# 32 latent tokens fewer in the dense expert path of each layer, gathered instead, with u and v rows side by side

## The chip, the cores and the metric

The kernel runs on one core of one Trainium2 chip. The metric is the device time of one execution, in microseconds, and less is better. All times are of this one core.

## The reference, cut to what matters

The reference is a stack of two layers over 512 latent tokens and 256 context tokens of 1024 features. Each layer has a token mixer (gated recurrences and short convolutions) and then an expert mixer. Only the expert mixer is touched here:

```python
cand = (s1[..., :, None] + s2[..., None, :]).reshape(bsz, t, PEER_HEADS, n_cand)
cidx = (i1[..., :, None] * N_KEYS + i2[..., None, :]).reshape(bsz, t, PEER_HEADS, n_cand)
top, pos = lax.top_k(cand, PEER_TOPK)
eidx = jnp.take_along_axis(cidx, pos, axis=-1)
gate = jax.nn.softmax(top, axis=-1).astype(h.dtype)
def block(args):
    hk, ek, gk = args
    act = jax.nn.gelu(jnp.einsum('ted,td->te', u[ek], hk), approximate=False)
    return jnp.einsum('te,ted->td', gk * act, v[ek])
```

Each token picks 8 x 16 = 128 of 16384 experts. An expert is one row of u and one row of v, of 1024 numbers each. For each picked expert the token's features are multiplied with the row of u, the sum goes through a GELU and is scaled with the gate, and that number scales the row of v. The sum over the 128 experts is added to the token's features. In the last layer the context does not pass the expert mixer, since nothing reads it any more.

## The kernel before, in words

Tokens are held transposed: 128 partitions of features, eight chunks, tokens along the free axis. `peer` (a layer's expert mixer) serves tokens in blocks of 128, in one of two ways.

The dense way computes all 16384 experts for the token, and multiplies those that it didn't pick with a gate of zero. Layer 0 does so for all four latent blocks (nt = 512 tokens) and layer 1 for three (nt = 384). Matrices are split into a high and a low part, so each product is three matmuls (lines 302 to 304 for u, in `experts_in`; 818 to 820 for v, in `dense`): 6144 matmuls of nt columns per layer. Each 512 KB tile of weights is loaded by SyncE (line 291), rounded by ScalarE to the high part (`whi`, line 293), and VectorE subtracts it for the low part (`wlo`, line 295). The gates of a block are built in `gates` out of one-hot matrices, in groups of 32 tokens: `oB` is built by VectorE for the first ND tokens of eight (line 757) and by ScalarE for the others (lines 761, 762), `oA` by VectorE (lines 765, 768), and small matmuls (line 773) join them. The result goes to DRAM (`gd`). Beside this stage some of the experts' activations are computed ahead (34 pairs of tiles in layer 0, 30 in layer 1) and parked in DRAM (`ad`). The dense stage then loads gates and parked activations, multiplies them (line 807), splits them (lines 810, 811), and adds the products with v to the residual (line 822).

The gathering way fetches only the picked rows. Layer 0 does so for the two context blocks and layer 1 for the last latent block. In `gather_block` partition p is token p, and slot e fetches the row of the e-th picked expert of each token: one indirect DMA of 128 rows of 4 KB, issued by GpSimd (line 854). A first loop over 128 slots fetches rows of u and takes the dot product with the token's features on VectorE (line 861). One GELU on ScalarE serves all slots. A second loop fetches rows of v and accumulates them on VectorE (line 870). Buffers are `gr` (3) and, in every fourth slot, `gs` (1). Buffers of `gs` come from a pool that opens behind the gate stage, so U0 = 96 says how many slots of the first context block may use `gr` alone and so start early, during the gate stage. At the end the sums are transposed by TensorE (line 875) and added to the residual (line 877).

The order of each engine's instructions is fixed when the program is built, by a scheduler that works from its own estimates. Dense and gathering work are interleaved on VectorE's queue by it. An engine executes its queue in order, so an instruction that waits holds up those behind it.

## Time and profile before

| what | value |
|---|---|
| median of 3 runs (lowest to highest) | 4181.68 us (4173.64 to 4183.18) |
| the profiled execution: time, and its span | 4183.52 us, 4181.8 us |
| TensorE matmuls busy | 3942.6 us (94%) |
| TensorE weight loads busy | 3419.5 us (82%) |
| VectorE busy | 3392.2 us (81%) |
| ScalarE busy | 1747.0 us (42%) |
| GpSimd busy | 1203.1 us (29%) |
| DMA moved | 984.54 MB, mean 235 GB/s |

The shares are means over the whole span, and the stages differ. The expert mixer of layer 0 has its top-k from about 600 us, its gate stage from 917, its dense stage from 1300 to 2419; in layer 1 the gate stage runs from 3015 to 3267 and the dense stage to 4125. The first stretch up to 600 us and that from 2440 to 2840 us are the token mixers. Weight loads overlap the matmuls. The DMA share is the mean busy share of the 16 DMA engines.

### The profile page before, as it was taken

The page shows a single profiled execution, that of the slowest core. Times are in us where ns is not written, and L with a number is a line of the kernel's source. Part 1 is how long each engine was busy: PE and PEld are TensorE (multiplying, and loading weights), DVE is VectorE, ACT ScalarE, POOL GpSimd, SP SyncE. Part 2 cuts the span into 40 slices and gives each one's busy share as a digit, 9 for nine tenths or more (in the row PEclk, how much of TensorE's full clock was granted, in tenths as well). Part 3 has the DMA queues.
Part 4 walks back from the last instruction along what each step waited for, and adds up shares of the span by engine and source line. Part 5 has one row for each costly group of instructions (what it writes and reads, how often), then busy time and mean ns, then how long its engine had stood idle before and what let it go on. Part 6 is the DMA issues. An engine that isn't in the chain of part 4 may idle for free.

```text
span 4181.8 us, 59060 instructions
## 1 busy us (share of the span) xinstructions
PE 3942.6 (94%) x21357; PEld 3419.5 (82%) x21357; DVE 3392.2 (81%) x6672; ACT 1747.0 (42%) x2919; POOL 1203.1 (29%) x924
## 2 busy tenths in 40 slices
PE   7999999999996999999999989989999999999995
PEld 4888868878885777877777768867999999999994
DVE  4766639989997999888888878758986688888886
ACT  4444332347774222222222245433599433333331
POOL 0211100033331244555555612210000024444443
PEclk9999999999998999999999999989999999999997
DMA  6444122379998899989989821112467679999996
GB/s 224 141 148 154 60 71 81 116 270 322 322 324 278 299 329 356 319 314 323 326 318 324 312 96 56 66 61 92 146 213 220 217 260 344 343 342 343 344 333 212
DMA packets 382164, 984.54 MB, mean 235 GB/s; under 512 B 30384, under 2 KB 161712, under 8 KB 377520
## 3 DMA queue, kind: packets, MB, share of 16 engines
q1 hardware_dynamic: 271280, 578.06, 40.1%
q0 software_dynamic: 110592, 402.70, 27.2%
q8 instruction: 169, 2.77, 0.3%
q14 instruction: 123, 1.01, 0.1%
HBM read 883.39 MB, written 97.26 MB: 235 GB/s over the span
## 4 chain that ended last, share of the span: by engine, by line
PE 50%; DVE 18%; issue 13%; DMA 10%; POOL 6%; ACT 2%; SPq 0%; POOLq 0%; DVEq 0%; ACTq 0%
PE pj L302 5%; PE p L820 5%; POOL gr L854 5%; PE pj L303 5%; PE pj L304 5%; PE p L818 5%; PE p L819 5%; PE p L302 4%; PE p L303 4%; PE p L304 4%; DMA gr<-in_v,picki 4%; DVE wlo L295 3%; PE gps L773 2%; DMA gr<-in_u,picki 2%; DVE acc L870 2%
## 5 line engine op out<-in xcount | busy, mean ns | idle before, releaser
L293 ACT ACTIVATE whi<-wraw 128x1024 fp32r<-128x1024 f32 x624 | 657.2, 1060 | 1266.8 <-PE p L819 568.7
L854 POOL DMA_INDIRECT gr<-in_u,picki x312 | 410.7, 1316 | 1545.7 <-DVE picki L828 634.9
L295 DVE TENSOR_TENSOR wlo<-wraw,whi 128x1024 fp32r<-128x1024 f32 x624 | 762.0, 1225 | 109.2 <-ACT whi L293 107.5
L818 PE MATMUL p<-Wh,whi 128*128 128x512 f32 (+1 forms) x2048 | 738.6, 366 | 38.5 <-ACT Wh L810 20.1
L820 PE MATMUL p<-Wh,wlo 128*128 128x512 f32 (+1 forms) x2048 | 747.5, 367 | 18.3 <-DVE wlo L295 18.1
L819 PE MATMUL p<-Wl,whi 128*128 128x512 f32 (+1 forms) x2048 | 749.1, 366 | 16.0 <-DVE Wl L811 15.9
L302 PE MATMUL p<-hxh,whi 128*128 128x512 f32 (+1 forms) x2048 | 751.7, 367 | 0.0
L303 PE MATMUL p<-hxl,whi 128*128 128x512 f32 (+1 forms) x2048 | 749.9, 366 | 0.0
L304 PE MATMUL p<-hxh,wlo 128*128 128x512 f32 (+1 forms) x2048 | 749.4, 367 | 0.0
L854 POOL DMA_INDIRECT gr<-in_v,picki x288 | 393.1, 1365 | 426.1 <-DVE acc L870 313.3
L818 PEld LDWEIGHTS p<-Wh,whi 128*128 128x128 f32 x2048 | 387.2, 190 | 89.0 <-ACT Wh L810 22.9
L820 PEld LDWEIGHTS p<-Wh,wlo 128*128 128x128 f32 x2048 | 388.1, 190 | 72.9 <-DVE wlo L295 32.4
L861 DVE SCALAR_TENSOR_TENSOR gr<-gr,htok 128x1024 f32<-128x1024 f32 x312 | 378.5, 1221 | 80.2 <-DMA gr<-in_u,picki 79.2
L819 PEld LDWEIGHTS p<-Wl,whi 128*128 128x128 f32 x2048 | 388.3, 190 | 64.1 <-DVE Wl L811 23.5
L304 PEld LDWEIGHTS p<-hxh,wlo 128*128 128x128 f32 x2048 | 386.3, 189 | 39.5 <-DVE wlo L295 0.6
L302 PEld LDWEIGHTS p<-hxh,whi 128*128 128x128 f32 x2048 | 386.2, 189 | 38.6
L303 PEld LDWEIGHTS p<-hxl,whi 128*128 128x128 f32 x2048 | 385.9, 188 | 38.8
L870 DVE SCALAR_TENSOR_TENSOR acc<-gr,gw,acc 128x1024 f32<-128x1024 f32 x285 | 365.4, 1282 | 54.5 <-DMA gr<-in_v,picki 52.7
L810 ACT ACTIVATE Wh<-A 128x1024 fp32r<-128x1024 f32 (+1 forms) x128 | 122.2, 955 | 368.9 <-DVE A L807 309.8
L302 PE MATMUL pj<-h512h,whi 128*128 128x512 f32 x640 | 262.0, 412 | 12.3 <-ACT whi L293 4.6
L773 PE MATMUL gps<-oA,oB 128*128 128x128 f32 x1792 | 253.3, 279 | 18.6 <-DVE oA L765 9.1
L773 PEld LDWEIGHTS gps<-oA,oB 128*128 128x128 f32 x1792 | 242.9, 193 | 31.6 <-ACT oB L762 8.4
(315 smaller groups left out, 6608.9 us busy)
## 6 DMA issues: line engine op xcount, KB each, us to landing
wraw<-in_ut SPq DMA_DIRECT2D x256, 512.0 KB
wraw<-in_vt SPq DMA_DIRECT2D x256, 512.0 KB
gd<-stg SPq DMA_DIRECT2D x28, 2048.0 KB
wmod<-in_w_mod SPq DMA_DIRECT2D x96, 512.0 KB
wraw<-in_w_in SPq DMA_DIRECT2D x64, 512.0 KB
gt<-gd SPq DMA_DIRECT2D x32, 1024.0 KB
gt<-gd SPq DMA_DIRECT2D x32, 768.0 KB
ad<-A SPq DMA_DIRECT2D x34, 512.0 KB
```

What stands on the lines that cost most here:

```text
L293: nc.scalar.activation(hi, raw, AF.Copy)
L295: nc.vector.tensor_tensor(lo, raw, hi.bitcast(F), op=OP.subtract)
L302: nc.tensor.matmul(out, wh[:, k], ah[:, k, :n], start=i == 0, stop=False)
L303: nc.tensor.matmul(out, wh[:, k], al[:, k, :n], start=False, stop=False)
L304: nc.tensor.matmul(out, wl[:, k], ah[:, k, :n], start=False, stop=i == KC - 1)
L773: nc.tensor.matmul(pt[:, s], B[:, s4 + s], A[:, s4 + s], start=True, stop=True)
L818: nc.tensor.matmul(pt, hi[:, j], wh, start=j == 0, stop=False)
L819: nc.tensor.matmul(pt, hi[:, j], wl, start=False, stop=False)
L820: nc.tensor.matmul(pt, lo[:, j], wh, start=False, stop=j == NG - 1)
L854: nc.gpsimd.indirect_dma_start(out=t, out_offset=None, in_=src, in_offset=bass.IndirectOffsetOnAxis(ap=eidx[:, e:e + 1], axis=0))
L861: nc.vector.scalar_tensor_tensor(u, u, 1.0, htok, op0=OP.mult, op1=OP.mult, accum_out=act[:, e:e + 1])
L870: nc.vector.scalar_tensor_tensor(acc, v, w[:, e:e + 1], acc, op0=OP.mult, op1=OP.add)
```

## The change

In each layer the last 32 latent tokens of the dense tokens (REST) leave the dense path: nt is 480 in layer 0 and 352 in layer 1. They are gathered in a further call of `gather_block`, behind the other blocks, four slots to an operation: partition 32 j + i holds token i and slot group j, so that 128 slots of 32 tokens are 32 operations. A matmul with `pack` (four stacked unit matrices) adds the four groups as it transposes.

For all gathers, u and v are laid side by side in DRAM, so one indirect DMA fetches 128 rows of 8 KB. There is one loop: fetch a slot, take the dot product, GELU and gate scale for this slot on ScalarE, and accumulate the previous slot. Buffers are two `gr` and two `gs` of 8 KB per partition. U0 is 24, ND is 3 instead of 4 (ScalarE builds five of eight rows of `oB`), and the last block's gate groups are three instead of four. In `dense` the two gate multiplications become one. Tile A has two buffers in layer 0. The store of x for the next layer comes behind the gathers. Some scratch tiles share the buffers of `wlo`, and the transposing matmul of the modulation writes two columns.

```diff
-ND = 4
+ND = 3
+REST = (32, 32)
-U0 = 96
+U0 = 24
...
-                nc.tensor.matmul(pm[:, j], part[:, j * P:(j + 1) * P], self.selm, start=True, stop=True)
+                nc.tensor.matmul(pm[:, j, 0:2], part[:, j * P:(j + 1) * P], self.selm[:, 0:2], start=True, stop=True)
...
-        nt = len(db) * P
+        r = REST[l]
+        nt = len(db) * P - r
...
-                    self.gates(kp, gd, n, ahead, *self.select(kp, tbs[b], 2))
+                    sel = self.select(kp, tbs[b], 2)
+                    nq = (nt - n * P) // 32
+                    self.gates(kp, gd, n, ahead, *sel, min(nq, P // 32))
+                    if nq < P // 32:
+                        e32 = kp.tile([P, PH * TOPK], I32, name="e32", tag="ri", bufs=1)
+                        self.eidx(sel, e32)
+                        for j in range(P // r):
+                            for dst, src in ((rest[0], e32), (rest[1], sel[2])):
+                                nc.sync.dma_start(dst[j * r:(j + 1) * r], src[P - r:, j * r:(j + 1) * r])
...
+                self.gather_block(l, cp, c2, hdx[0, P - r:], *rest, TC + nt, r, 0)
                 if not last:
                     self.xd = self.dram.tile([P, KC, TX], F, name="xd")
...
-        A = ap.tile([P, 2, nt], F, name="A", tag="A", bufs=3)
+        A = ap.tile([P, 2, nt], F, name="A", tag="A", bufs=2 if l == 0 else 3)
...
-                for t in range(2):
-                    av = A[:, t].rearrange("p (c t) -> p c t", t=32)
-                    nc.vector.tensor_tensor(av, av, gt[:, :, j % 4 + t, :], op=OP.mult)
+                av = A.rearrange("p i (c t) -> p i c t", t=32)
+                gv = gt[:, :, j % 4:j % 4 + 2, :].rearrange("p c i t -> p i c t")
+                nc.vector.tensor_tensor(av, av, gv, op=OP.mult)
...
-    def gather_block(self, l, cp, c2, b, hd, eidx, gate, n0):
+    def gather_block(self, l, cp, c2, hd, eidx, gate, t0, n, n0):
         nc, a = self.nc, self.a
-        S = PH * TOPK
+        D = KC * P
+        S = PH * TOPK * n // P
...
+        def fetch(e):
+            if e < n0 or e % 4 < 2:
+                t = cp.tile([P, 2, D], F, name="gr", tag="gr", bufs=2)
             else:
+                t = c2.tile([P, 2, D], F, name="gs", tag="gs", bufs=2)
+            nc.gpsimd.indirect_dma_start(out=t.rearrange("p a d -> p (a d)"), out_offset=None, in_=a[f"uv{l}"],
                                          in_offset=bass.IndirectOffsetOnAxis(ap=eidx[:, e:e + 1], axis=0))
...
+        def dot(e, t):
+            nc.vector.scalar_tensor_tensor(t[:, 0], t[:, 0], 1.0, htok, op0=OP.mult, op1=OP.mult,
+                                           accum_out=act[:, 0, e:e + 1])
+            self.gelus[1] = nc.scalar.activation(act[:, 1, e:e + 1], act[:, 0, e:e + 1], AF.Gelu).ins
+            nc.scalar.activation(act[:, 2, e:e + 1], act[:, 1, e:e + 1], AF.Copy, scale=gate[:, e:e + 1])
...
+        prev = None
         for e in range(S):
+            t = fetch(e)
+            dot(e, t)
+            if prev is not None:
+                add(e - 1, prev)
+            prev = t
+        add(S - 1, prev)
...
+                    nc.tensor.matmul(pt, acc[:, c * P:(c + 1) * P], self.pack, start=True, stop=True)
...
-        d[f"u{l}"] = peer_u[l]
-        d[f"v{l}"] = peer_v[l]
+        d[f"uv{l}"] = np.concatenate([peer_u[l], peer_v[l]], axis=1)
```

Three places of the order tell what the diff can't. The first is VectorE's queue at the end of layer 0's dense stage. `resx<-p` is a dense addition to the residual, `acc<-gr` or `acc<-gs` an accumulation of a slot, `resc<-accT` the addition of a finished context block. Before (the second of these dense additions is the layer's last):

```order
L822 SCALAR_TENSOR_TENSOR resx<-p_18008,mod_108,resx 128x512
L295 TENSOR_TENSOR wlo<-wraw,whi 128x1024
L870 SCALAR_TENSOR_TENSOR acc<-gr,gw,acc 128x1024 x2
L822 SCALAR_TENSOR_TENSOR resx<-p_18040,mod_108,resx 128x512
L295 TENSOR_TENSOR wlo<-wraw,whi 128x1024
L870 SCALAR_TENSOR_TENSOR acc<-gr,gw,acc 128x1024
L870 SCALAR_TENSOR_TENSOR acc<-gs,gw,acc 128x1024
L877 SCALAR_TENSOR_TENSOR resc<-accT,mod_108,resc 128x128 x2
```

Now the same place (line 879 is the dot product, 889 the accumulation, 836 the dense addition):

```order
L836 SCALAR_TENSOR_TENSOR resx<-p_17965,mod_113,resx 128x480
L889 SCALAR_TENSOR_TENSOR acc<-gr,act,acc 128x1024
L879 SCALAR_TENSOR_TENSOR gs,act<-gs,htok 128x1024
L889 SCALAR_TENSOR_TENSOR acc<-gs,act,acc 128x1024
L836 SCALAR_TENSOR_TENSOR resx<-p_17997,mod_113,resx 128x480
L879 SCALAR_TENSOR_TENSOR gs,act<-gs,htok 128x1024
L889 SCALAR_TENSOR_TENSOR acc<-gs,act,acc 128x1024
L879 SCALAR_TENSOR_TENSOR gr,act<-gr,htok 128x1024
L889 SCALAR_TENSOR_TENSOR acc<-gr,act,acc 128x1024
L879 SCALAR_TENSOR_TENSOR gr,act<-gr,htok 128x1024
L889 SCALAR_TENSOR_TENSOR acc<-gr,act,acc 128x1024
```

Two accumulations stood behind the last dense addition; now 45 dot products and 45 accumulations do, in this pattern, 13 of the second context block and 32 of the new block.

The second place is TensorE's queue at the same point. `p` is a dense product, `accT` the transpose of a gathered sum, `nst` the statistics of the next layer's first norm over all 512 latent tokens, `pj` its first projection. Before:

```order
L820 MATMUL p_18040<-Wh,wlo 128x512
L237 MATMUL nst<-sq,ones_70 32x512 x7
L875 MATMUL accT<-ident,acc 128x128
L237 MATMUL nst<-sq,ones_70 32x512
L875 MATMUL accT<-ident,acc 128x128
L245 MATMUL nst_19969<-cols,npart 128x1 x4
L875 MATMUL accT<-ident,acc 128x128 x3
L221 MATMUL rb<-ident,n0r 128x128 x4
L875 MATMUL accT<-ident,acc 128x128
L302 MATMUL pj<-h512h,whi 128x512 x2
```

Now:

```order
L834 MATMUL p_17997<-Wh,wlo 128x480
L904 MATMUL accT<-ident,acc 128x128 x8
L906 MATMUL accT<-pack,acc 128x32 x2
L241 MATMUL nst<-sq,ones_70 32x512
L906 MATMUL accT<-pack,acc 128x32
L241 MATMUL nst<-sq,ones_70 32x512
L906 MATMUL accT<-pack,acc 128x32
L241 MATMUL nst<-sq,ones_70 32x512
L906 MATMUL accT<-pack,acc 128x32
```

The norm's statistics followed the last dense matmul; now the transposes of both gathered blocks stand between, and the norm's statistics follow the new block's.

The third place is the end of layer 1's dense stage on VectorE. Before:

```order
L822 SCALAR_TENSOR_TENSOR resx<-p_34461,mod_109,resx 128x384
L870 SCALAR_TENSOR_TENSOR acc<-gr,gw,acc 128x1024 x2
L822 SCALAR_TENSOR_TENSOR resx<-p_34493,mod_109,resx 128x384
L870 SCALAR_TENSOR_TENSOR acc<-gr,gw,acc 128x1024
L870 SCALAR_TENSOR_TENSOR acc<-gs,gw,acc 128x1024
L870 SCALAR_TENSOR_TENSOR acc<-gr,gw,acc 128x1024 x3
```

Now:

```order
L836 SCALAR_TENSOR_TENSOR resx<-p_34490,mod_114,resx 128x352
L908 SCALAR_TENSOR_TENSOR resx<-accT,mod_114,resx 128x32
L836 SCALAR_TENSOR_TENSOR resx<-p_34522,mod_114,resx 128x352
L908 SCALAR_TENSOR_TENSOR resx<-accT,mod_114,resx 128x32
L836 SCALAR_TENSOR_TENSOR resx<-p_34554,mod_114,resx 128x352
L215 TENSOR_SCALAR fv<-nst_35884 128x4
```

Accumulations stood behind the last dense addition; now both gathered blocks are finished ahead of it, and the final norm follows at once.

## Rows read from the trace of the kernel before

**Rows 1.** Busy time by stretch: stretch, its length, engines with instructions, TensorE clock, DMA share, GB/s.

```profile
917.00:1300.00 383.00, 362.90 (x2055) 312.80 (x2053) 351.14 (x710) 306.85 (x707) 128.33 (x101) 0.99 0.95 318
1300.00:2419.00 1119.00, 1054.67 (x4524) 853.25 (x4524) 972.57 (x1292) 297.50 (x292) 548.21 (x388) 0.98 0.90 319
3015.00:3267.00 252.00, 252.00 (x1726) 251.81 (x1726) 186.00 (x386) 235.61 (x546) 0.00 (x0) 1.00 0.67 207
3267.00:3395.00 128.00, 124.08 (x701) 121.95 (x700) 108.15 (x319) 45.65 (x49) 0.00 (x0) 0.99 0.62 206
3395.00:4125.00 730.00, 720.26 (x4112) 711.10 (x4111) 645.60 (x818) 241.58 (x255) 326.99 (x246) 1.00 0.92 337
4125.00:4151.00 26.00, 0.00 (x0) 0.00 (x0) 17.98 (x14) 0.00 (x0) 12.92 (x11) 0.54 0.76 247
4151.00:4182.00 31.00, 15.85 (x40) 5.27 (x40) 9.21 (x22) 8.62 (x13) 0.00 (x0) 0.67 0.18 68
```

**Rows 2.** Timeline of TensorE: start us, duration us, instruction; layer 0, layer 1, gate stage.

```profile
1699.73 0.39 PE L302 MATMUL p<-hxh,whi 128*128 128x512 f32 x1
...
1701.09 0.39 PE L302 MATMUL p<-hxh,whi 128*128 128x512 f32 x1
...
3700.14 0.33 PE L302 MATMUL p<-hxh,whi 128*128 128x384 f32 x1
...
3701.01 0.33 PE L304 MATMUL p<-hxh,wlo 128*128 128x384 f32 x1
...
3018.82 2.84 PE L773 MATMUL gps<-oA,oB 128*128 128x128 f32 x24
```

**Rows 3.** Timeline of VectorE: two dot products, then an accumulation and what follows it.

```profile
3707.71 1.22 DVE L861 SCALAR_TENSOR_TENSOR gr<-gr,htok 128x1024 f32<-128x1024 f32 x1
...
3708.85 1.22 DVE L861 SCALAR_TENSOR_TENSOR gr<-gr,htok 128x1024 f32<-128x1024 f32 x1
...
1560.25 1.28 DVE L870 SCALAR_TENSOR_TENSOR acc<-gr,gw,acc 128x1024 f32<-128x1024 f32 x1
1561.44 1.22 DVE L295 TENSOR_TENSOR wlo<-wraw,whi 128x1024 fp32r<-128x1024 f32 x1
```

**Rows 4.** DMA queues in 917:1300, 1300:2419, 3395:4125 (with slices), 4125:4151: packets, MB, share.

```profile
q0 software_dynamic: 14633, 53.25, 39.9%
...
q0 software_dynamic: 55850, 203.40, 51.7%
q1 hardware_dynamic: 42284, 152.90, 37.8%
...
GB/s 322 362 324 394 320 321 368 324 348 395 264 356 378 308 375 315 317 375 331 324 408 271 353 386 304 355 346 314 357 352 316 398 282 341 385 296 330 344 296 240
q0 software_dynamic: 35092, 127.80, 47.9%
q1 hardware_dynamic: 31392, 117.85, 44.0%
...
q0 software_dynamic: 1772, 6.43, 76.4%
```

**Rows 5.** Groups by line and shape: one-hot rows on ScalarE in 3015:3267; small activations, whole span.

```profile
L762 ACT ACTIVATE oB<-oB,gt,gtn 128x128 f32<-128x128 f32 x192 | 83.2, 529 | 0.0
L761 ACT ACTIVATE oB<-iota,gt 128x128 f32<-128x128 f32 x184 | 60.5, 434 | 0.0
...
L213 ACT ACTIVATE or<-os x8: 205/206/210, 187.8 to 2779.6; 128x6 f32<-128x6 f32 x4, 128x4 f32<-128x4 f32 x4
```

**Rows 6.** Timeline of VectorE behind the last dense matmul: first, last slot; last addition.

```profile
4120.67 1.31 DVE L870 SCALAR_TENSOR_TENSOR acc<-gr,gw,acc 128x1024 f32<-128x1024 f32 x1 [0.53 <-DMA gr<-in_v,picki]
...
4149.72 1.28 DVE L870 SCALAR_TENSOR_TENSOR acc<-gs,gw,acc 128x1024 f32<-128x1024 f32 x1
...
4162.43 0.35 DVE L877 SCALAR_TENSOR_TENSOR resx<-accT,mod,resx 128x128 f32<-128x128 f32 x1 [0.89 <-PE accT L875]
```

**Rows 7.** Groups by line and shape: the modulation's transposing matmul.

```profile
L191 PE MATMUL pmod<-selm,mpart 128*128 128x128 f32 x192 | 30.9, 283 | 2.7 <-ACT mpart L189 2.7
```

More of the change, by code (lines that the diff above doesn't have):

```diff
@@ L90, in setup @@
             nc.vector.tensor_copy(self.selm[q:q + 2, 0:2], self.ident[0:2, 0:2])
+        self.pack = c.tile([P, 32], F, name="pack")
+        for q in range(0, P, 32):
+            nc.vector.tensor_copy(self.pack[q:q + 32], self.ident[0:32, 0:32])
         self.res = self.streams()
@@ L227, in norm_close @@
         t0, nt, pp = nm
-        part = self.wp.tile([P, nt], F, name="npart", tag=f"np{nt}", bufs=1)
+        part = self.wp.tile([P, nt], F, name="npart", tag="wlo", bufs=3)
         self.nc.scalar.activation(part, pp, AF.Copy)
@@ L667, in peer @@
             ad = dr.tile([n_ahead, P, 2, nt], F, name="ad")
-            hd = dr.tile([len(gb), P, KC * P], F, name="hd")
+            hd = dr.tile([NCB, P, KC * P], F, name="hd")
+            hdx = hd if last else dr.tile([1, P, KC * P], F, name="hdx")
             sd = dr.tile([len(gb), PH, P, 2, P], F, name="sd")
@@ L673, in peer, with pick_bufs @@
             cp = self.pool(f"pc{l}", stack=es, side="right")
-            def pick_bufs(pool):
-                return [pool.tile([P, PH * TOPK], dt, name="pick" + n) for n, dt in (("i", I32), ("g", F))]
+            def pick_bufs(pool, n=PH * TOPK):
+                return [pool.tile([P, n], dt, name="pick" + k + str(n)) for k, dt in (("i", I32), ("g", F))]
             picks = [pick_bufs(cp) for _ in range(early)]
+            rest = pick_bufs(cp, r)
             with ExitStack() as es2:
@@ L685, in peer @@
                 self.nms = None, None
-                if last:
-                    self.norm_mod(nmx, l, 1, 0, *hx, hd=hd, b0=NB - NCB - 1)
-                else:
+                self.norm_mod(nmx, l, 1, 0, *hx, hd=hdx, b0=NB - NCB - (2 if last else 1))
+                if not last:
                     hcb = kp.tile([P, 2, KC, TC], R, name="hcb", tag="big", bufs=2)
                     hc = [hcb[:, 0], hcb[:, 1]]
-                    self.norm_mod(nmx, l, 1, 0, *hx)
                     self.norm_mod(nmc, l, 1, 1, *hc, hd=hd)
@@ L727, in peer @@
                 self.dense(l, es2, ap, gd, ad, hx, nt)
+                for n, b in enumerate(gb):
+                    if n >= early:
+                        picks.append(pick_bufs(c2))
+                        self.late_top(c2, sd[n], *picks[n])
+                    self.gather_block(l, cp, c2, hd[1 if last else n], *picks[n], b * P, P, U0 if n < early else 0)
+                self.gather_block(l, cp, c2, hdx[0, P - r:], *rest, TC + nt, r, 0)
                 if not last:
@@ L731, in peer, with gates @@
                         nc.sync.dma_start(self.xd[:, c], self.res.x[:, c])
-                for n, b in enumerate(gb):
-                    if n >= early:
-                        picks.append(pick_bufs(c2))
-                        self.late_top(c2, sd[n], *picks[n])
-                    self.gather_block(l, cp, c2, b, hd[n], *picks[n], U0 if n < early else 0)
-    def gates(self, kp, gd, n, ahead, i1, i2, gate):
+    def gates(self, kp, gd, n, ahead, i1, i2, gate, nq):
         nc = self.nc
@@ L749, in gates @@
         nc.scalar.activation(tn, tg, AF.Copy, scale=-1.0)
-        for q in range(P // 32):
+        for q in range(nq):
             stg = kp.tile([P, P, 32], F, name="stg", tag="big", bufs=2)
@@ L822, in dense, with eidx @@
                 nc.vector.scalar_tensor_tensor(dst, pt, self.mod[l][:, 5 * KC + c, 0:1], dst, op0=OP.mult, op1=OP.add)
+    def eidx(self, sel, out):
+        i1, i2, _ = sel
+        self.nc.vector.scalar_tensor_tensor(i1, i1, 128.0, i2, op0=OP.mult, op1=OP.add)
+        self.nc.vector.tensor_copy(out, i1)
     def pick(self, pool, tb, nh, eidx, gate):
-        nc = self.nc
-        i1, i2, g = self.select(pool, tb, nh)
-        nc.vector.scalar_tensor_tensor(i1, i1, 128.0, i2, op0=OP.mult, op1=OP.add)
-        nc.vector.tensor_copy(eidx, i1)
-        nc.vector.tensor_copy(gate, g)
+        sel = self.select(pool, tb, nh)
+        self.eidx(sel, eidx)
+        self.nc.vector.tensor_copy(gate, sel[2])
     def late_top(self, cp, sd, eidx, gate):
@@ L864, in gather_block @@
-        nc.vector.tensor_tensor(w, w, gate, op=OP.mult)
-        for e in range(S):
-            v = fetch(a[f"v{l}"], e)
-            if e == 0:
-                nc.vector.tensor_scalar(acc, v, w[:, e:e + 1], None, op0=OP.mult)
-            else:
-                nc.vector.scalar_tensor_tensor(acc, v, w[:, e:e + 1], acc, op0=OP.mult, op1=OP.add)
-        s = 1 if b < NCB else 0
+        def dot(e, t):
[3 more added lines that the diff above has]
+            nc.scalar.activation(act[:, 2, e:e + 1], act[:, 1, e:e + 1], AF.Copy, scale=gate[:, e:e + 1])
@@ new lines, in add @@
+        def add(e, t):
+            w = act[:, 2, e:e + 1]
+            if e == 0:
+                nc.vector.tensor_scalar(acc, t[:, 1], w, None, op0=OP.mult)
+            else:
+                nc.vector.scalar_tensor_tensor(acc, t[:, 1], w, acc, op0=OP.mult, op1=OP.add)
+        prev = None
+        for e in range(S):
+            t = fetch(e)
[4 more added lines that the diff above has]
+        add(S - 1, prev)
+        s = 1 if t0 < TC else 0
```

32 lines of the change are left out of this document (13 added, 19 removed).

## The prediction

> **What bounds the kernel now.** I read the busy time by stretches first, because the stages have different limits [rows 1]. The stretches are the gate stage of layer 0 (917 to 1300 us), its dense stage (1300 to 2419), the gate stage of layer 1 (3015 to 3267), its dense stage (3267 to 4125) and the end. In both dense stages TensorE is busy 94 to 99%, so it looks like the bound. But the DMA engines are at 0.90 to 0.92 and VectorE at 87 to 88% in the same stretches: three lanes are nearly full, and work taken off one must land on another. In the gate stage of layer 0 the DMA share is the highest of all, 0.95. In that of layer 1 TensorE and ScalarE (236 of 252 us) are both full. The last rows of the group show what an unfinished gather costs: from 4125 to 4151 TensorE does nothing.
>
> Then I read the steps from one instruction to the next. Six dense matmuls of 512 columns start within 1.36 us (1699.73 to 1701.09) and five of 384 within 0.87 (3700.14 to 3701.01) [rows 2]: steps of 227 and 174 ns. So 128 columns cost 53 ns and 32 columns 13.2 ns. On VectorE a dot product takes 1.14 us to the next instruction and an accumulation 1.19 [rows 3], so one slot (dot and add) costs 2.33 us.
>
> **The change, part by part.** I price against the profiled execution, 4183.5 us (span 4181.8); the median of the runs is 1.8 us below it.
>
> *TensorE, dense.* 6144 dense matmuls in each layer become 32 columns narrower: 2 x 6144 x 13.2 ns = 162 us of TensorE time. That is the gain if TensorE were the only bound. Below I ask stage by stage what is late next.
>
> *Added gathers.* 768 gathers of 512 KB become 448 of 1 MB: bytes rise from 403 to 470 MB. VectorE gets 64 slots more, 64 x 2.33 = 149 us.
>
> *Gate stage, layer 0 (383 us).* One group of 32 tokens of 16 falls away. TensorE: 1009 expert matmuls at 227 ns and 1024 small ones at 0.118 us [rows 2] are 350 us; after, 992 at 213.8 ns and 960 small ones are 325. The order holds 120 dot products ahead of the stage's end before and 28 slots now, so about 30 MB of gathers in place of 63; 53 MB of them took 39.9% of the stretch [rows 4]. So the DMA engines, full before, have room. ScalarE gets busier: five one-hot rows of eight instead of four, 300 pairs in place of 256, each 0.9 us by its two mean durations [rows 5], +40; fewer copies, -5; the 56 small operations of the early slots at 0.2 us [rows 5], +12: 354 of busy time. ScalarE is late next. I take 360 us, **-23** (from 345 to 383).
>
> *Dense stage, layer 0 (1119 us).* TensorE: 4512 matmuls x 213.8 ns = 965 us instead of 1024. VectorE: 973 us [rows 1], plus 79 dots and minus 36 adds that stand in this stage, +47; the two gate multiplications become one and all tiles are shorter, about -17: 1003. DMA: the gathers took 51.7% for 203 MB, or 2.98 us per MB-slot of 1.049 MB; the fastest slice of layer 1 moves 408 GB/s, or 2.57 us [rows 4]. 215 slots are 553 to 641 us; the other queue's 423 us lose about 9. Sum 967 to 1055; at a share of 0.95, the fullest stretch seen, 1018 to 1110. I take 1075, nearer the upper end, since 2.87 and 2.98 come from stretches of this very kind: **-44**. The lower bound is VectorE's 1003 at 97%, 1035.
>
> *The tail of layer 0.* This is the largest term. Behind the last dense addition VectorE's order has 45 whole slots (13 of the second context block, 32 of the new one), where it had two additions. TensorE's order has nothing between the last dense matmul and the transposes of these slots: the new block belongs to latent tokens, so the next layer's norm over all 512 waits for it. Nothing covers this. From below a slot costs VectorE's 2.33, 105 us. From above: in the bare tail of layer 1, 16 half-size slots took 29.05 us, 1.82 each [rows 6]; twice that is 3.63, 163 us. By the engines alone 6.43 MB at 76.4% of 26 us [rows 4] make 3.24. I take 2.9, between VectorE's floor and that: **+130**. Behind it the eight transposes and additions come one after another, 4151 to 4163 in [rows 6], +12, which ran beside the norm before; and TensorE idles, with its granted clock at 0.54 in the idle stretch and 0.67 in the next [rows 1], so I add 5: **+17**.
>
> *Gate stage, layer 1 (252 us).* Both TensorE and ScalarE are full. TensorE loses a twelfth of the small matmuls and 13.2 ns on the others but is given 137 more expert matmuls: it stays near 250. ScalarE gets 28 more pairs; their two durations add to 0.96 us but overlap by a fifth [rows 5], +21; with six more weight casts it comes to about 260 busy. I take **+12** (0 to +20).
>
> *Dense stage, layer 1 (858 us).* TensorE: 4608 matmuls x 160.8 ns = 741. VectorE: 754 us [rows 1] and 32 dots, 45 adds more, 10 weight splits and some columns less: 816. DMA: the first 128 us, until the late top-k lets the first gather go, run at 0.62 and stay so. Then 160 slots at 2.57 to 2.87 are 411 to 459, and the other queue's 323 us [rows 4] fall to about 305: 716 to 764, at 0.95 754 to 804, and 882 to 932 with the first 128. I take 900: **+42**. The floor is VectorE's 816 at 97%, 841.
>
> *The end.* In the order of layer 1 all slots stand ahead of the last dense addition, so the 26 us with idle TensorE and most of the eight transposes go: 57 us shrink to about 21, **-36**.
>
> *Small edits.* The modulation's transposing matmul writes 2 columns instead of 128: 192 records of 31 us busy [rows 7], beside a TensorE that is full in the mixers, **-8** (0 to -16). Two small ScalarE operations per slot, 0.2 us each [rows 5], lie on an engine that is 27% busy in the dense stages, and table loads stay at 26: zero; their cost if ScalarE stood late is in rival B. One wait is new there: the GELU of a slot waits for its dot, and the weight casts queue behind it. The store of x for the next layer moves behind the gathers: zero, since its reader comes a mixer later. Sharing of scratch tiles: zero. In layer 0 tile A has two buffers instead of three; inside the range of the dense stage.
>
> Sum: -23 - 44 + 130 + 17 + 12 + 42 - 36 - 8 = +90; 4183.5 + 90 = 4273.5, and 4272 against the median.
>
> **A rule against the row.** The rows show half-size gathers served at 1.49 us each (half of 2.98) with up to four in flight [rows 4], so whatever each transfer costs by itself is mostly covered already. The Trainium skill (DMA: Bandwidth & Descriptors, Anatomy of one DMA) puts a GpSimd DMA at about 2.0 us plus its bytes over 436 GB/s; by an estimate from its figures one 1 MB transfer takes 4.4 us where two of 512 KB take 6.4. By that rule the gathers lose a third, and the sum would be that of rival A; the trace so far bears it out only in part, since the fixed part is hidden there.
>
> **The rivals.** A, *merged transfers make the DMA engines cheap* and VectorE sets the pace: dense 1035 and 845 us, a slot of the tail at 2.33 us. -23 - 84 + 105 + 12 + 8 - 13 - 36 - 8 = -39: 4143, faster. For it: nobody has seen a 1 MB gather here, and one slice reaches 408 GB/s. Against: whole stretches ran at 2.87 to 2.98. It decides below about 2.5 us per slot.
>
> B, *the slots run at the ceiling*: dense 1114 and 932, the tail at 3.33 us per slot (150 us), because four buffers and a chain of DMA, dot, two ScalarE steps and add give too little ahead. -23 - 5 + 150 + 17 + 12 + 74 - 36 - 8 = +181: 4363. For it: the tail price of 3.24 to 3.63, and ScalarE's new waits ahead of the weight casts.
>
> C, *the two sides cancel*, within 0.3%: a dense stage as in A with a tail as forecast, about 4182.
>
> That the change does not do what it says is excluded by the order: 448 gathers, matmuls of 480 and 352 columns.
>
> **How the numbers follow.** Forecast 0.50, A 0.22, B 0.21, C 0.07. A measurement of this kernel tells about 0.3% (12.5 us) from no change. So faster 0.22, same 0.07, slower 0.71. The forecast's own range is 4205 to 4335; the range for 8 in 10 reaches to the prices of A and B, 4140 to 4365, which leaves out the outer halves of both.
>
> **What would show it.** Right: in layer 0 some 105 to 163 us with TensorE idle behind its last dense matmul while VectorE alternates dots and adds; DMA share at or above 0.93 in both dense stages; layer 1's dense stage longer than 858 us although its matmul step falls to 161 ns; no idle TensorE at the end. Wrong: a 1 MB slot served in under 2.5 us, dense stages under 1035 and 845 us, a layer 0 tail under 100 us, or a matmul step that stays at 174 ns.

## The result, and the profile after

The changed kernel takes 4391.41 us (median of 4 runs, 4383.59 to 4395.10), the kernel before 4177.66 (4168.38 to 4183.18): ratio 1.0512, 95% interval 1.0486 to 1.0538. It is slower by 214 us; the forecast was +90, and 4391 lies above the range. The profiled executions are 4183.5 and 4389.8 us. By stage, in us of these two (a stage ends with its last gate matmul or its last dense addition):

| stage | before | after | difference | forecast |
|---|---|---|---|---|
| up to the first gate matmul of layer 0 | 919.6 | 941.3 | +22 | -4 |
| gates, layer 0 | 380.2 | 356.1 | -24 | -23 |
| dense, layer 0 | 1119.2 | 1110.6 | -9 | -44 |
| from there to the first gate matmul of layer 1 | 599.9 | 768.1 | +168 | +143 |
| gates, layer 1 | 247.7 | 261.5 | +14 | +12 |
| dense, layer 1 | 858.3 | 926.7 | +68 | +42 |
| end | 56.9 | 23.6 | -33 | -36 |

(The forecast's -8 for the modulation is halved between the two mixers; +143 is the tail's 130, the restart's 17 and -4.) Every miss of more than 1 us is to the slow side.

The busy time by stretches of the kernel after, columns as in [rows 1]: gates of layer 0, two parts of its dense stage, its tail and the restart, gates of layer 1, its dense stage (up to the first slot, while slots run, behind the last slot), the end.

```profile
941.06:1297.16 356.10, 338.55 (x1963) 303.02 (x1961) 261.54 (x490) 330.99 (x829) 28.82 (x19) 0.98 0.74 240
1297.00:1800.00 503.00, 415.53 (x1731) 342.98 (x1732) 470.25 (x739) 157.05 (x301) 130.34 (x97) 0.91 0.94 349
1800.00:2408.00 608.00, 606.63 (x2793) 522.74 (x2791) 521.86 (x606) 226.23 (x417) 189.09 (x123) 1.00 0.89 330
2408.00:2555.00 147.00, 3.80 (x8) 1.46 (x8) 111.29 (x143) 23.67 (x91) 63.75 (x42) 0.51 0.85 310
2555.00:2593.00 38.00, 25.41 (x74) 10.30 (x75) 16.41 (x33) 15.28 (x28) 1.85 (x5) 0.66 0.23 83
3176.00:3437.30 261.30, 255.85 (x1774) 252.60 (x1772) 167.05 (x309) 250.64 (x592) 0.00 (x0) 0.99 0.65 206
3437.00:3576.00 139.00, 121.39 (x724) 119.36 (x723) 114.65 (x323) 46.82 (x51) 4.51 (x4) 0.91 0.59 191
3576.00:4331.00 755.00, 657.05 (x3707) 627.63 (x3706) 688.89 (x842) 282.22 (x553) 230.00 (x156) 0.94 0.94 363
4331.00:4364.00 33.00, 33.00 (x213) 32.39 (x211) 14.66 (x24) 8.51 (x10) 0.00 (x0) 1.00 0.24 78
4364.00:4387.70 23.70, 8.34 (x32) 3.58 (x28) 6.63 (x14) 7.02 (x11) 0.00 (x0) 0.69 0.24 89
```

The reader is to see three things. In the gates of layer 0 the DMA share is 0.74 where it was 0.95: with two buffers, no others open yet and U0 = 24, the gathers stop at 28 slots. In both dense stages TensorE now waits: in the first 503 us of layer 0's it is busy 83%, with VectorE at 93%, and then 99.8% with VectorE at 86%; in layer 1's it is busy 87% while slots run and 100% behind them. And in 147 us of layer 0 TensorE has nothing to do but eight transposes (3.8 us). Before, the two parts of layer 0's dense stage were nearly alike for TensorE, 93 and 95%:

```profile
1299.60:1800.00 500.40, 464.42 (x1999) 376.06 (x1997) 453.44 (x679) 135.41 (x130) 204.41 (x144) 0.97 0.89 318
1800.00:2419.00 619.00, 590.43 (x2527) 477.19 (x2527) 519.13 (x614) 162.27 (x162) 343.79 (x245) 0.98 0.90 320
```

In that tail, VectorE's timeline (start us, duration us, instruction, idle time before it and what ended it) repeats this pattern:

```profile
2410.85 1.22 DVE L879 SCALAR_TENSOR_TENSOR gr<-gr,htok 128x1024 f32<-128x1024 f32 x1
2411.99 0.08 DVE L879 DVE_READ_ACCUMULATOR gr<-gr,htok 128x1 f32 x1
2412.67 1.28 DVE L889 SCALAR_TENSOR_TENSOR acc<-gr,act,acc 128x1024 f32<-128x1024 f32 x1 [0.60 <-ACT act L882]
2413.88 1.22 DVE L879 SCALAR_TENSOR_TENSOR gr<-gr,htok 128x1024 f32<-128x1024 f32 x1
...
2452.05 1.23 DVE L879 SCALAR_TENSOR_TENSOR gr<-gr,htok 128x1024 f32<-128x1024 f32 x1 [1.76 <-DMA htok<-hdx]
```

Dot to dot is 3.03 us (2410.85 to 2413.88). The program's loop takes the dot of slot e ahead of the addition of slot e - 1, but the order pairs each addition with its own dot, so VectorE waits 0.60 us for the GELU and the scaling. Where one block follows the other it also waits for the sum's transposes and for the new block's token rows (2452.05).

### The profile page after: what moved, and what is told of

Same layout as the page of the kernel before. It is cut to its first block, busy times and chain, and to the rows that moved or that the text cites. A ratio compares the mean times of both kernels' runs of the same rounds, so it can differ in the third digit from the quotient of the medians.

```text
span 4387.7 us, 59003 instructions
## 1 busy us (share of the span) xinstructions
PE 3882.4 (88%) x21277; PEld 3389.6 (77%) x21277; DVE 3464.9 (79%) x6605; ACT 1965.5 (45%) x3956; POOL 823.9 (19%) x604
## 4 chain that ended last, share of the span: by engine, by line
PE 38%; issue 26%; DVE 16%; POOL 10%; DMA 7%; ACT 4%; POOLq 0%; SPq 0%; DVEq 0%; ACTq 0%
POOL gr L874 5%; POOL gs L874 5%; PE pj L306 5%; PE pj L307 5%; PE pj L308 5%; DMA gr<-in_uv,picki 4%; PE p L308 3%; PE p L306 3%; PE p L307 3%; PE gps L787 2%; DVE wlo L299 2%; PE p L834 2%; PE p L832 2%; PE p L833 2%; DVE acc L889 2%
## 5 line engine op out<-in xcount | busy, mean ns | idle before, releaser
L832 PE MATMUL p<-Wh,whi 128*128 128x480 f32 (+1 forms) x2048 | 745.0, 368 | 109.0 <-ACT Wh L824 77.1
L834 PE MATMUL p<-Wh,wlo 128*128 128x480 f32 (+1 forms) x2048 | 747.5, 367 | 42.6 <-DVE wlo L299 42.3
L833 PE MATMUL p<-Wl,whi 128*128 128x480 f32 (+1 forms) x2048 | 743.2, 364 | 24.6 <-DVE Wl L825 24.5
L308 PE MATMUL p<-hxh,wlo 128*128 128x480 f32 (+1 forms) x2048 | 734.1, 358 | 11.8 <-DVE wlo L299 11.6
L306 PE MATMUL p<-hxh,whi 128*128 128x480 f32 (+1 forms) x2048 | 730.8, 357 | 15.5 <-ACT whi L297 15.5
L307 PE MATMUL p<-hxl,whi 128*128 128x480 f32 (+1 forms) x2048 | 730.5, 357 | 0.0
L874 POOL DMA_INDIRECT gr<-in_uv,picki x236 | 355.5, 1506 | 1952.5 <-DVE acc L889 710.8
L874 POOL DMA_INDIRECT gs<-in_uv,picki x212 | 305.2, 1440 | 841.8 <-DVE acc L889 569.9
L889 DVE SCALAR_TENSOR_TENSOR acc<-gr,act,acc 128x1024 f32<-128x1024 f32 x231 | 295.5, 1279 | 24.3 <-ACT act L882 23.7
L889 DVE SCALAR_TENSOR_TENSOR acc<-gs,act,acc 128x1024 f32<-128x1024 f32 x212 | 271.1, 1279 | 13.3 <-ACT act L882 12.0
```

Of the source, the lines that this page charges most:

```text
L306: nc.tensor.matmul(out, wh[:, k], ah[:, k, :n], start=i == 0, stop=False)
L307: nc.tensor.matmul(out, wh[:, k], al[:, k, :n], start=False, stop=False)
L308: nc.tensor.matmul(out, wl[:, k], ah[:, k, :n], start=False, stop=i == KC - 1)
L832: nc.tensor.matmul(pt, hi[:, j], wh, start=j == 0, stop=False)
L833: nc.tensor.matmul(pt, hi[:, j], wl, start=False, stop=False)
L834: nc.tensor.matmul(pt, lo[:, j], wh, start=False, stop=j == NG - 1)
```

## The experiments

Times are medians, and each ratio is against the kernel before, measured beside it. Stage times are from one profiled execution of each kernel.

### Which half of the change carries the price

**norest**: the new block taken out, everything else kept.

```diff
-REST = (32, 32)
+REST = (0, 0)
...
-        act = cp.tile([P, 3, S], F, name="act", tag="act", bufs=1)
+        act = cp.tile([P, S], F, name="act", tag="act", bufs=1)
...
-            sc = cp.tile([P, 2, P], F, name="csc", tag="csc", bufs=2)
+            sc = cp.tile([P, 2, P], F, name="csc", tag="csc", bufs=1)
...
-        self.pick(cp, tb, 2, eidx, gate)
+        self.pick(cp, tb, 1, eidx, gate)
```

> The changed kernel with all latent blocks dense again (512 and 384 columns, 256 and 128 slots), u and v still side by side, one loop, U0 = 24. Three small tiles of the gathers are made smaller so that it fits. Theory F (the new block carries the price): no bare tail (4 accumulations stand behind the last dense addition instead of 44) and 32 slots fewer in each layer; the start stays 20 us later than before: 4200, within 30 us. Theory M (the side-by-side rows with their late start carry it: the gather lanes stand idle in the second half of layer 0's gate stage, so 34 whole slots move into the dense stage): layer 0's dense stage grows to 1200 us or more, total 4300 or more.

4299.01 us, ratio 1.0285 (1.0249 to 1.0320). Theory F falls: with the block gone, 120 of the 214 us stay. Theory M has the total about right but not the place: layer 0's dense stage is 1137 us, under its 1200. The largest piece is layer 1's dense stage: 928 us, with the slots and the columns of before, where it took 858; next come layer 1's gates, 286 us instead of 248.

**drop**: the new block's gathers alone left out.

```diff
-                self.gather_block(l, cp, c2, hdx[0, P - r:], *rest, TC + nt, r, 0)
```

> The changed kernel without the gathers of the new block: its 32 tokens of each layer get no expert output at all (the dense part stays at 480 and 352 columns). Theory F (full lanes: in both dense stages DMA engines and VectorE are full, so each slot costs its whole service, and the tail of layer 0 is bare): 32 slots of the tail at 147 us / 45 slots = 3.27 us are 105 us, the block's own transposes about 11, and 32 slots in layer 1 at 8 packets per DMA engine x 338 ns / 0.94 = 2.9 us are 92 us: 4391 - 208 = 4183, within 30 us. Theory O (the order paces: TensorE waits for what the scheduler put too early on VectorE's queue, not for the slots themselves): layer 1 gains under 40 us, so 4240 or more.

4244.75 us, ratio 1.0145 (1.0106 to 1.0183). The time from layer 0's last dense addition to layer 1's gates falls by 120 us, but layer 1's dense stage only from 927 to 900: theory O. 32 slots fewer bring that stage only 27 us, so something else paces it. The slots left out all stood late: 15, 67 and 119 slots stand ahead of dense addition 32, 64 and 96, nearly as in the change (15, 66, 117), so the first three quarters of the stage are as crowded as they were, and behind the last slot TensorE runs alone for 168 us.

**rest_old**: the block without the side-by-side rows, and with the gate split, the early slots and the scratch buffers of before. The edit shown is that of the two loops.

```diff
-            nc.gpsimd.indirect_dma_start(out=t.rearrange("p a d -> p (a d)"), out_offset=None, in_=a[f"uv{l}"],
...
+        for e in range(S):
+            u = fetch(a[f"u{l}"], e, n0)
...
+        for e in range(S):
+            v = fetch(a[f"v{l}"], e)
```

> The new block alone: 480 and 352 dense columns and the block of 4 slots per operation last, but u and v fetched apart by two loops with the small buffers of before, ND = 4, U0 = 96, the norms' partial sums in buffers of their own. In the order 97 half-size slots stand behind the last dense addition of layer 0 and 95 behind that of layer 1 (before: 2 and 14). Theory F (the block carries its price whatever the layout): two bare tails of about 165 and 160 us, less 59 and 68 us of dense matmuls, 37 of the gate stages and 29 of the old tail, 11 more for the token rows of the new block: 4179 + 139 = 4318, within 35 us. Theory M (the layout side by side carries it, the block itself is cheap): 4200 or less.

4393.13 us, ratio 1.0524 (1.0508 to 1.0541): 75 us above theory F's figure, and as slow as the change. Dense stage and tail of layer 0, then of layer 1, columns as above:

```profile
1283.00:2331.00 1048.00, 999.43 (x4523) 851.76 (x4521) 916.56 (x1199) 291.85 (x288) 510.74 (x363) 0.98 0.90 324
2331.00:2520.00 189.00, 3.79 (x8) 1.46 (x8) 127.00 (x141) 1.77 (x3) 120.12 (x95) 0.51 0.80 272
3357.00:4169.00 812.00, 778.27 (x4771) 764.73 (x4769) 711.76 (x1054) 280.60 (x301) 306.36 (x228) 1.00 0.88 319
4169.00:4352.00 183.00, 3.80 (x8) 1.46 (x8) 123.36 (x137) 0.23 (x1) 114.12 (x93) 0.51 0.80 270
```

Here the dense stages are 71 and 46 us shorter than before, and TensorE is busy 95 and 96%. Not all of that is the narrower columns: fewer half-size slots run in these stages too (361 instead of 390, and 224 instead of 242). For 98 and 96 half-size slots wait until TensorE has done, and cost 189 and 183 us. Together with norest: the block's slots cost more than its matmuls, whether they are squeezed in or left behind. Everything in the change but the block costs 120 us (norest), the block alone 216, both together 214: the prices do not add.

### What paces the dense stage of layer 1

TensorE's timeline of norest in layer 1, one of its waits:

```profile
3698.19 0.34 PE L839 MATMUL p<-Wl,whi 128*128 128x384 f32 x1
3701.62 0.69 PE L838 MATMUL p<-Wh,whi 128*128 128x384 f32 x1 [3.10 <-ACT Wh L830]
3702.11 0.53 PE L840 MATMUL p<-Wh,wlo 128*128 128x384 f32 x1
3702.43 0.53 PE L838 MATMUL p<-Wh,whi 128*128 128x384 f32 x1
...
3707.16 0.34 PE L838 MATMUL p<-Wh,whi 128*128 128x384 f32 x1
3707.34 0.34 PE L839 MATMUL p<-Wl,whi 128*128 128x384 f32 x1
```

TensorE waits 3.10 us for Wh, which waits for the gate multiplication on VectorE, behind slots. Then the matmuls step at 0.32 us instead of 0.174 up to 3707.16; from 3701.60 to 3706.90 the granted clock is 0.50, the lower level of 1.2 GHz:

```profile
3701.60:3706.90 5.30, 5.28 (x16) 5.28 (x17) 5.30 (x7) 2.15 (x4) 1.41 (x1) 0.50 1.03 419
```

So what follows this wait costs time as well as the wait. From 3482 to 4100, while slots run, most of TensorE's waits in norest end with VectorE's weight split (wlo) or with Wh, as the one above (waited for: us in total, times, longest):

```profile
PE p L840 <- DVE wlo L299: 30.0, 23, 2.0
PE p L838 <- ACT Wh L830: 24.0, 10, 3.1
```

These two are 54 of 68 us. The weight casts on ScalarE waited for weight transfers only 4 times there, 3.5 us in all, so late weights are not the cause.

In norest's order 15, 66, 118 and 128 of the 128 slots stand ahead of dense addition 32, 64, 96 and 128: four 1 MB buffers hold twice the slots that four of 512 KB did, and the order sets slots denser than before (there 99 half-size slots, so 49.5 whole ones, by addition 64). **nr_l1b3** takes one buffer away, in layer 1 only.

```diff
-            if e < n0 or e % 4 < 2:
+            if e < n0 or (e % 4 < 2 if l == 0 else e % 3 < 2):
...
-                t = c2.tile([P, 2, D], F, name="gs", tag="gs", bufs=2)
+                t = c2.tile([P, 2, D], F, name="gs", tag="gs", bufs=1 if l else 2)
```

> The kernel of the run norest with three slot buffers of 1 MB in layer 1 instead of four. Same slots, same bytes, same columns; only the order spreads the 128 slots of layer 1 evenly over its dense stage (12, 49, 87, 128 slots by dense addition 32, 64, 96, 128, instead of 15, 66, 118, 128). Theory P (pace: four 1 MB buffers let the scheduler set slots so densely that VectorE, in order, hands TensorE its operands late, while at the end TensorE runs alone): layer 1's dense stage falls from 928 us to about 870, total 4299 - 58 = 4241, within 20 us. Theory D (the DMA engines at 0.95 to 0.97 are the limit, and the bytes are the same): 4299, within 12 us.

4244.72 us, ratio 1.0179 (1.0140 to 1.0217); the dense stage is 865 us instead of 928. Theory P holds and D falls: the bytes are the same. One buffer less also means fewer bytes in flight at a time; since norest hardly waited for weights, that is not where the 63 us come from. Norest's stretches (first fence) beside those of nr_l1b3:

```profile
3700.00:3800.00 100.00, 88.66 (x465) 86.05 (x466) 92.67 (x112) 36.35 (x71) 28.69 (x22) 0.93 0.96 366
3800.00:3900.00 100.00, 88.55 (x485) 84.84 (x483) 92.82 (x112) 36.70 (x72) 29.92 (x22) 0.98 0.97 381
...
4100.00:4200.00 100.00, 100.00 (x580) 99.75 (x579) 53.54 (x62) 34.29 (x36) 0.00 (x0) 1.00 0.49 170
```

```profile
3700.00:3800.00 100.00, 97.45 (x555) 95.74 (x555) 87.73 (x106) 40.12 (x69) 24.85 (x18) 1.00 0.89 342
3800.00:3900.00 100.00, 96.65 (x538) 95.06 (x537) 88.62 (x106) 38.10 (x68) 23.19 (x17) 0.97 0.91 339
...
4100.00:4217.00 117.00, 115.60 (x661) 113.96 (x660) 105.75 (x126) 45.85 (x84) 33.03 (x21) 1.00 0.85 320
```

Norest runs VectorE at 93% with a starved TensorE, then TensorE alone with VectorE at 54%; spread evenly, both stay near full.

**af_l1b3**: the same edit on the changed kernel.

> The changed kernel with three slot buffers in layer 1 instead of four. In the order 128 instead of 160 slots then stand ahead of layer 1's last dense addition, 12, 49, 87, 128 by addition 32, 64, 96, 128, and 32 behind it. Theory P (VectorE's order paces TensorE): the dense stage falls from 927 us to about 815 (the run nr_l1b3 had 865 with 384 columns), and the 32 slots become a bare tail of 32 x 3.27 = 105 us and 12 us of transposes: 4391 - 112 + 117 = 4396, within 20 us; the slots cost the same either way. Theory D (bytes limit the dense stage): it stays above 880 us and the total is above 4450.

4425.80 us, ratio 1.0590 (1.0569 to 1.0610). The dense stage falls to 829 us, close to theory P's 815. D's 880 was no fair test, since 32 slots with their bytes leave the stage. The fair comparison is drop: the same 128 slots in the stage, the same columns, four buffers, and 900 us. So of the 98 us gained some 71 come from the even order, and pace sets this stage here too, although the weight casts wait longer for transfers than in the change (61 us in all, where it was 27). But the tail is 124 us, 3.87 us per slot with three buffers, and the total is 30 us above the expectation. In the changed kernel layer 1's 160 slots cost the same or more wherever they stand.

### The size of a transfer

**two_dma**: a slot of the changed kernel fetched by two transfers.

```diff
-            nc.gpsimd.indirect_dma_start(out=t.rearrange("p a d -> p (a d)"), out_offset=None, in_=a[f"uv{l}"],
-                                         in_offset=bass.IndirectOffsetOnAxis(ap=eidx[:, e:e + 1], axis=0))
+            for k in range(2):
+                nc.gpsimd.indirect_dma_start(out=t[:, k], out_offset=None, in_=a[f"{'uv'[k]}{l}"],
+                                             in_offset=bass.IndirectOffsetOnAxis(ap=eidx[:, e:e + 1], axis=0))
```

> The changed kernel with each 1 MB slot fetched by two transfers of 512 KB, from u and from v, into the same buffer; one loop, four buffers and all else as changed. If bytes set a slot's price (a packet of 8192 bytes took 338 ns in layer 1, two of 4096 took 2 x 178 before), the bare tail of layer 0 stays at 3.2 to 3.5 us per slot and the total within 20 us of 4391. If each transfer has a price of its own that four buffers don't hide (the Trainium skill's fixed part of about 2 us), a slot of the tail takes 5 us or more and the total is 4500 or more.

4416.55 us, ratio 1.0580 (1.0563 to 1.0597), 25 us above the change, 5 beyond the first theory's margin and far from the other's 4500. In its tail 34 slots take 113 us, 3.32 each:

```profile
2433.00:2546.00 113.00, 3.80 (x8) 1.46 (x8) 84.95 (x111) 19.04 (x70) 75.77 (x62) 0.51 0.85 299
```

This compares with 147 / 45 = 3.27 in the change. But each tail holds one change of blocks, which weighs more among fewer slots. The 32 slots of the new block alone, from the first dot to the end of the last addition, take 103.1 us in the change and 99.2 us in two_dma, with VectorE's regular step at 3.03 us in both (change first):

```profile
2452.05:2555.10 103.05, 1.43 (x3) 0.55 (x3) 78.59 (x100) 17.21 (x65) 42.41 (x28) 0.50 0.81 298
2447.17:2546.40 99.23, 0.00 (x0) 0.00 (x0) 77.73 (x97) 17.20 (x65) 67.85 (x56) 0.50 0.84 303
```

So merging two transfers saves nothing here. By stages two_dma loses 7 us at the start, 4 and 14 us in layer 0's gates and dense stage, and 34 us in layer 1's dense stage (961), whose order is denser still (74 slots by dense addition 64, 66 in the change); it gains 36 us behind layer 0's last dense addition, where 34 slots stand instead of 45.

### Earlier slots, another order of blocks

**u64**

```diff
-U0 = 24
+U0 = 64
```

> U0 64 instead of 24: 46 instead of 28 slots stand in the order of layer 0 ahead of the gate stage's end, and 31 instead of 44 accumulations behind its last dense addition. Theory M (the late start costs): the tail of layer 0 loses 13 x 3.27 = 43 us and the dense stage nothing: 4348, within 15 us. Rival (the gate stage is full of ScalarE work, early slots lengthen it by what they save behind): 4391, within 12 us.

4376.28 us, ratio 1.0462 (1.0425 to 1.0499): 15 us better, between the two expectations. The time from the last dense addition to the next gates falls by 48 us, but the gates take 370 us (+14) and the dense stage 1130 (+19): two thirds are given back. The start (+4) and layer 1's dense stage (+9) take most of the rest in the profiled execution, which was the slowest of four (4388 us), so the 15 us are not located further.

**rest_mid**: the new block ahead of the late block.

```diff
+                    if n == early:
+                        self.gather_block(l, cp, c2, hdx[0, P - r:], *rest, TC + nt, r, 0)
...
-                self.gather_block(l, cp, c2, hdx[0, P - r:], *rest, TC + nt, r, 0)
```

> The new block's gathers stand ahead of the late context block in layer 0 and ahead of the latent block in layer 1, instead of last. The number of slots is the same. In layer 1 the first slot then stands at dense addition 0 instead of 21, because its experts are known before the late top-k; in layer 0 49 context slots stand behind the last dense addition. Theory F (DMA engines full): layer 1 fills the 139 us in which the DMA share was 0.59, worth (0.94 - 0.59) x 139 = 49 us; in layer 0 the norm of the latent tokens no longer waits for the tail, and whatever of the mixer runs ahead of the context is gained, 0 to 60 us: 4285 to 4342. Rival (only the order's pace counts, the tail stays bare since the mixer needs the context at once): 4380 or more.

4393.62 us, ratio 1.0504 (1.0467 to 1.0541): nothing gained; the rival holds. In layer 1 the slots do start at once, but the dense stage is 923 us against 927 and the gates take 274 instead of 262: an idle DMA engine was not the limit. In layer 0 TensorE's queue shows why the tail stays bare:

```profile
2431.70 1.22 PE L307 MATMUL pj<-h512l,whi 128*128 128x512 f32 x2 [0.49 <-DVE h512l L288]
2576.87 0.47 PE L905 MATMUL accT<-ident,acc 128*128 128x128 f32 x1 [143.95 <-DVE acc L890]
```

The next mixer's latent projection begins under the tail, but the transposes of the context sum, which have high priority, come right after its first matmuls, and everything else queues behind them.

### Small edits

**scratch**

```diff
-        part = self.wp.tile([P, nt], F, name="npart", tag="wlo", bufs=3)
+        part = self.sm.tile([P, nt], F, name="npart", tag=f"np{nt}", bufs=1)
...
-        tmp = self.wp.tile([P, 3, 8], F, name="tmp", tag="wlo", bufs=3)
+        tmp = self.sm.tile([P, 3, 8], F, name="tmp", tag="mpart", bufs=1)
```

The norms meant are those of the mixers and the last one.

> The changed kernel with the partial sums of the mixers' norms and the small table of the setup in buffers of their own, as before, instead of sharing the three buffers of wlo. Theory S (the first projections of the program wait for a wlo buffer that a norm holds): the 20 us by which layer 0's top-k starts later than before go: 4371, within 10 us. Rival (the two-column matmul of the modulation, or its scratch tile, sets the first order): 4391, within 8 us.

4374.43 us, ratio 1.0490 (1.0451 to 1.0529), and layer 0's gates start at 918.6 us instead of 941.3: theory S. The waits of VectorE in the first 100 us of the changed kernel (engine, line, waited for: us in total, times, longest) hold the row

```profile
DVE wlo L299 <- ACT npart L233: 4.3, 1, 4.3
```

It has no counterpart before: a weight split of the first projections waits until a norm has let go of its buffer. The run shows that the sharing costs 23 us up to the gates; this row shows 4.3 of them, and the others are not traced to single waits.

**nr_nd4**, on norest:

```diff
-ND = 3
+ND = 4
```

> The kernel of the run norest with ND = 4: VectorE builds four one-hot rows of eight again, ScalarE four instead of five. If ScalarE is late in the gate stage of layer 1 (286 us here, 248 before), 48 pairs less at 0.8 us give 38 us there and nothing in layer 0, whose gate stage has VectorE near full: 4262, within 12 us. Rival (TensorE full in layer 1's gate stage, ScalarE's share hidden): 4299, within 12 us.

4269.25 us, ratio 1.0238 (1.0200 to 1.0276), as expected in total but not by its reason. The gates of layer 1, norest's row first:

```profile
3057.00:3343.00 286.00, 285.34 (x1910) 284.33 (x1909) 182.99 (x338) 275.53 (x648) 0.00 (x0) 1.00 0.63 206
```

```profile
3045.00:3293.00 248.00, 248.00 (x1703) 247.80 (x1703) 182.65 (x377) 231.65 (x538) 0.00 (x0) 1.00 0.65 208
```

The stage is 38 us shorter, but TensorE is full in both and has 207 matmuls less in it; they follow in the dense stage, which grows by 28. Layer 0 does the same: -35 and +30. What is left, 10 and 5 us, and 8 us in the mixers between make up the 21 us between the two profiled executions.

### Towards a faster version

**c3**, on norest: ND = 4, U0 = 64, the own buffers of scratch, and three slot buffers in both layers.

> No new block (512 and 384 columns), u and v side by side, but ND = 4, U0 = 64, three slot buffers in both layers, and the norms' partial sums in buffers of their own. If the theories P, S and the one on ScalarE hold and add up: 4299 - 58 - 36 - 20 = 4185, and up to 20 us less by 17 more slots that run in layer 0's gate stage: 4165 to 4185, beside 4179 of the kernel before. If the DMA engines or 1 MB transfers limit: 4240 or more.

4198.54 us, ratio 1.0070 (1.0044 to 1.0096). That is 14 us above the expectation's upper end. Most of the loss is recovered, and yet the side-by-side rows bring nothing against before. Layer 0's gates and dense stage take 1533 us together where they took 1499, and layer 1's 1140 where they took 1106; the start (-11) and the end (-31) do not make up for it. nr_l1b3's 865 us for layer 1's dense stage are not reached (892), for the matmuls that ND = 4 moves out of the gates follow in it, as in nr_nd4.

**b_small**: the kernel before with two edits of the change.

```diff
-                nc.tensor.matmul(pm[:, j], part[:, j * P:(j + 1) * P], self.selm, start=True, stop=True)
+                nc.tensor.matmul(pm[:, j, 0:2], part[:, j * P:(j + 1) * P], self.selm[:, 0:2], start=True, stop=True)
...
-                for t in range(2):
-                    av = A[:, t].rearrange("p (c t) -> p c t", t=32)
-                    nc.vector.tensor_tensor(av, av, gt[:, :, j % 4 + t, :], op=OP.mult)
+                av = A.rearrange("p i (c t) -> p i c t", t=32)
+                gv = gt[:, :, j % 4:j % 4 + 2, :].rearrange("p c i t -> p i c t")
+                nc.vector.tensor_tensor(av, av, gv, op=OP.mult)
```

> The kernel before with two of the change's small edits alone: the modulation's transposing matmul writes two columns, and the two gate multiplications of a pair are one. The first starts layer 0's gate stage 5 to 11 us earlier (the run c3 had it 11 us ahead of before); the second takes about 0.2 us of VectorE per pair, 128 pairs, in stages where VectorE is at 88%: 0 to 15 us. So 4150 to 4170 beside the runs of before with it, ratio 0.994 to 0.999. Rival (all hidden): ratio 1.000.

4167.72 us, ratio 0.9983 (0.9971 to 0.9994): a little faster than both kernels, by less than the 0.3% that the prediction called distinguishable, but its interval leaves out 1. The gates of layer 0 start 4 us earlier.

## Why the prediction was wrong

The direction was right, and so were the gate stages (-23 and +12; measured -24 and +14) and the end (-36; -33). Four steps failed, all to the slow side; they make 112 of the 116 us by which the profiled executions differ from the forecast.

*"Sharing of scratch tiles: zero."* It cost 17 us in the median and 23 at the first gate matmul (scratch). I looked for work that hides it in the stages around the change, and this cost arises at the start of the program. Not priced at all were the transposes and stores of the new block's token rows in layer 0's norm: between 590 and 640 us the changed kernel falls 11 us further behind, and norest, which has none of them, doesn't. Of these 34 us 12 are made up before the first gate matmul (+22).

*"I take 1075, nearer the upper end"* for layer 0's dense stage: 1111, its upper bound. I added up each lane over the whole stage and took the fullest. But the stage has two halves with different bounds: VectorE 93% and TensorE 83% up to 1800 us, where the late top-k and the first slots crowd VectorE's queue, then TensorE 99.8%. Slack in one half can't serve the other, since the order is fixed. TensorE's own term was short too: its matmuls were busy for 1022 us, not 965, with a granted clock of 0.91 in the first half, where it waits, and 1.00 in the second. This is read from the trace of after; no run isolates it.

*"I take 2.9"* for a slot of the tail: 147 / 45 = 3.27, inside the bounds of 2.33 and 3.63. (The upper one was read short: the 16 starts within 29.05 us are 15 steps, 1.94 us each and 3.87 a pair.) VectorE's 2.33, 0.08 for reading the dot's sum and the wait of 0.60 for ScalarE make the 3.03 of the regular pattern but for 0.02; the rest is the change of blocks and late transfers. I had priced ScalarE's two steps at zero in the dense stages and did not ask about them in the tail, where nothing else stands between. So the tail is 147 instead of 130, and with 8 us more behind it this makes +168 instead of +143.

*"I take 900: +42"* for layer 1's dense stage: 927. I made the DMA engines its bound, at a share of 0.95. The share was 0.94, and 927 lies within its bounds of 882 to 932. But nr_l1b3 moves the same bytes in 63 us less than norest, drop takes a fifth of the slots away for 27, and af_l1b3 serves drop's slots in 71 us less. So the stage is paced by VectorE's queue, which hands TensorE its operands late where slots stand too densely, with a lower clock on top (0.94 while slots run, 1.00 before the change). Transfers have a part that no run isolates: in the changed kernel the weight casts on ScalarE wait 27 us for weights while slots run (46 us before, beside a TensorE 99% busy). With all 160 slots no run has a dense stage under 923 us.

Rival B came nearest in its number (4363). For the tail its reason held in part: its 3.33 us per slot counted the two ScalarE steps in the chain, and 3.27 was measured. For the dense stages it is turned round: four 1 MB buffers did not leave too little ahead, they let the order set too much ahead. Rival A's price was wrong: a slot of the tail took 3.27 us, not 2.33.

The rule of the Trainium skill (DMA: Bandwidth & Descriptors, Anatomy of one DMA) would, by an estimate from its figures, have two transfers of 512 KB cost 2.0 us more than one of 1 MB. two_dma doesn't agree: the new block's 32 slots took 99.2 us with two transfers each and 103.1 with one. With four buffers in flight nothing of a fixed part was left to save, as the trace before suggested; no run here has one transfer alone in flight.

What the change set out to buy did exist in part: rest_old shows 71 and 46 us less in the dense stages, with fewer slots in them as well. Its price, 32 more slots per layer for VectorE and the DMA engines, was larger in every arrangement tried.

## What to carry to other kernels

Where three engines are near full and their orders are fixed, count the work of each in the parts of a stage, and see where the order puts it: the same slots with the same bytes cost 63 us more when they were set too densely. More bytes in flight is not free: here larger buffers let the scheduler crowd VectorE's queue. Ask of each shared buffer who waits for it when nothing else runs, at the start and in a tail.

## What was not expected of the hardware

After a wait of 3.10 us TensorE ran 5.3 us at a granted clock of 0.50 (17 matmuls at 0.32 us instead of 0.174), so this wait cost some 2.5 us more than its length. And the half-size slots of a bare tail took 1.91 to 1.93 us each in rest_old, 3.8 per pair, where a whole slot of 1 MB took 3.27. The gain is not the size of the transfer, since two transfers per slot in the same loop were no slower (99.2 us for 32 slots, against 103.1). One loop with four 1 MB buffers also holds twice as much in flight; the runs do not separate the two.
